# The end of a top-k spread over all 128 partitions, and its mask moved by four transfers

## The chip, the cores and the metric

The kernel runs on one core of a Trainium2 chip. The metric is the device time of one execution in microseconds (us); the median over runs is compared.

## The reference

One step of a decoder layer for 512 prompt tokens and for 32 new tokens of 8 sequences (4 each, the "samples") that have 1024 cached keys. Two attention branches read the same normed input and are merged by gates; a feed-forward network follows. The change is in branch A, for the samples:

```
rel   = relu(einsum('bthe,bse->bths', q_i, k_i))
score = einsum('bth,bths->bts', w_i, rel) * IDX_DIM**-0.5
score = where(causal, score, -inf)
_, idx = top_k(score, 256)        # at ties the lower index wins
s = einsum('btcgd,btncd->btcgn', qg, kv_a[idx][..., 0]) * HEAD_DIM**-0.5
p = softmax(where(valid, s, -inf));  o = einsum('btcgn,btncd->btcgd', p, kv_a[idx][..., 1])
```

The kernel gathers nothing: it makes a mask over all 1056 keys of a row (1024 cached and 32 new ones), 0 for a chosen key and -1e30 for any other, adds it to the logits and takes the softmax over all.

## The kernel before, in words

The program is written as streams of small pieces, and a scheduler with a timeline of its own sets the order of the instructions on each engine from them. That order is fixed in the program: each engine takes its instructions in turn, and one that waits holds all behind it. In the stretch that matters (160 to 585 us of the span) three streams run side by side:

- **heads**: branch B and then branch A for the prompt, in units of one head and 128 query rows with 128, 256, 384 or 512 keys (a unit is named by its keys below). A unit of branch B is a product on PE into the PSUM bank `z` (L902), two sigmoids on ACT (`g` and `b`, L906, L907), a running product on DVE along `g` (L909), a product on POOL (L910), transposes on PE into `tp` (L825), copies on ACT and DVE (L828, L829) and the value product on PE (L838).
- **samples**: branch B for the samples in two groups of four sequences, then branch A. A group of branch B turns and splits keys (L992, L997, L998), makes logits on PE (L1021) and sums their parts into `zr` (`half` on ACT, L969; sum on DVE, L971). When the logits of the last keys are there, `weights` adds a mask to `zr` (L1045, DVE), takes sigmoids (L1047, L1048, ACT), a running product over 1056 keys (L1050, DVE) and a product (L1051, POOL); PE turns `zr` (L1058), ACT and DVE split it (L1065, L1066), and the value products follow (L1089), whose pages are split by ACT (L1082) and by DVE or POOL (L1083). Branch A for the samples comes last (`dsa_sample`): in `products` the mask is added to the logits by a matmul with the selector `rowsel` (L1149).
- **dense**: projections with weights in two parts, three matmuls to a product (L464), into the PSUM bank `mm`, emptied by ACT (`rowy`, L500). The weights are split by ACT (L116) and POOL (L119).

The banks `z` and `mm` exist once each: whoever wants one waits until the reader of the last value is done. SP issues the page loads (`kb`, `vb`, L375), the weight loads (L106) and the loads of the heads, in turn.

**The top-k.** The score `score_s` lies on 32 partitions, one row of 1056 keys each. Four transfers lay it out as `score4` on 128 partitions, 264 keys each (L591). Thirty-two rounds find the least chosen score bit by bit: a count per partition on DVE (L596), a matmul with `group` into `z` that adds the four counts of a row (L598), and two small operations on DVE (L600, L605 or L607). The streams interleave with these rounds. The end (L610 to L620) goes back to `score_s` on 32 partitions: which keys equal the least score (L612), which are greater and how many (L613), how many places are left (L614), a running count of the equal ones (L615), those of them that fit (L616), the sum (L617), and the mask in two pieces (L618 and L620). The mask is written with the cached keys in another order, so that `products` reads 256 neighbouring elements.

## Time and profile before

| what | value |
|---|---|
| median of 3 runs | 1070.34 us (1068.96 to 1074.01) |
| the profiled execution, its own time | 1067.42 us |
| its span, first to last instruction | 1065.6 us |
| busy: PE, DVE, ACT, POOL | 92%, 70%, 50%, 44% of the span |
| PE busy from 160 to 585 us | 386.31 of 425 us |

All times of instructions are from the profiled execution, in us from the start of its span. A row of a timeline has the start, the duration, the engine, the line, the operation, what it writes and reads, and in brackets the idle time of its engine before it and what ended that. PE is TensorE's matmuls, PEld its weight loads, DVE VectorE, ACT ScalarE, POOL GpSimd, SP the engine that issues most transfers. Matmuls overlap: what a matmul costs PE is the distance between starts. The granted clock of TensorE is given as a share of full speed.

### The profile page before, as it was taken

What the parts mean: (1) busy time and instruction counts of PE and PEld (TensorE: products, weight loads), DVE (VectorE), ACT (ScalarE), POOL (GpSimd) and SP (SyncE); (2) the same over time, 40 slices, a digit from 0 to 9 for tenths busy, and PEclk for the clock granted to TensorE, in tenths of its full rate; (3) what the DMA queues carried; (4) which work ended last, traced back from release to release, by engine and by line L of the source; (5) the groups of instructions that cost most, each with busy time, mean ns of one, the idle gap of its engine ahead of it and who ended that gap; (6) DMA issues with size and microseconds to landing.
All of it is one profiled execution on the core that took longest, in us unless ns stands there. A gap on an engine that the chain in (4) does not pass through costs nothing.

```text
span 1065.6 us, 20642 instructions
## 1 busy us (share of the span) xinstructions
PE 984.7 (92%) x7446; PEld 931.0 (87%) x7446; DVE 740.7 (70%) x1441; ACT 531.2 (50%) x1020; POOL 469.9 (44%) x413
## 2 busy tenths in 40 slices
PE   6899998787989996999999799979999999999995
PEld 5899998776669996888888799979999999999995
DVE  4468995798997786578784976787787876513233
ACT  6234535574556564677785544534444444423223
POOL 4555545226763236652635834411323232545441
PEclk9999999998999998999998999989999999999998
DMA  9775547886767765864525663223432341223222
GB/s 269 181 205 169 152 121 228 250 253 174 228 209 242 223 188 165 256 218 144 193 72 181 201 179 90 71 71 89 119 100 83 97 119 43 75 88 90 83 82 85
DMA packets 184704, 162.15 MB, mean 152 GB/s; under 512 B 13338, under 2 KB 148058, under 8 KB 183578
## 3 DMA queue, kind: packets, MB, share of 16 engines
q1 hardware_dynamic: 176410, 140.00, 45.5%
q0 software_dynamic: 1872, 10.75, 2.9%
q10 hardware_dynamic: 6320, 10.08, 2.9%
q8 instruction: 59, 0.97, 0.4%
q14 instruction: 43, 0.35, 0.1%
HBM read 133.37 MB, written 22.01 MB: 146 GB/s over the span
## 4 chain that ended last, share of the span: by engine, by line
PE 52%; DVE 11%; issue 7%; POOL 5%; DMA 4%; ACT 2%; SPq 1%; ACTq 0%; DVEq 0%; POOLq 0%
PE mm L464 8%; PE ffB L1553 8%; PE acc L1607 6%; PE ffC L1553 5%; PE ffA L1553 5%; POOL wl L119 4%; PE z L1607 3%; PE mm L1607 3%; PE acc L1021 2%; PE ts L992 2%; PE acc L1089 2%; DVE g L909 1%; DMA vb<-in_cache_kv_b 1%; PE tp L825 1%; PE tp L838 1%
## 5 line engine op out<-in xcount | busy, mean ns | idle before, releaser
L119 POOL TENSOR_TENSOR wl<-wst,wh 128x512 fp32r<-128x512 f32 (+2 forms) x198 | 228.8, 1177 | 193.8 <-ACT wh L116 193.8
L464 PE MATMUL mm<-xh,wh 128*128 128x256 f32 (+2 forms) x484 | 145.7, 301 | 9.3 <-ACT rowy L500 5.5
L464 PE MATMUL mm<-xh,wl 128*128 128x256 f32 (+2 forms) x484 | 141.6, 293 | 2.4 <-POOL wl L119 2.4
L464 PE MATMUL mm<-xl,wh 128*128 128x256 f32 (+2 forms) x484 | 142.5, 294 | 0.0
L116 ACT ACTIVATE wh<-wst 128x1024 fp32r<-128x1024 f32 (+3 forms) x99 | 88.6, 895 | 103.0 <-PE z L1607 42.1
L227 POOL TENSOR_TENSOR wl<-wst,wh 128x512 fp32r<-128x512 f32 x40 | 59.9, 1519 | 164.4 <-ACT wh L224 164.4
L464 PEld LDWEIGHTS mm<-xh,wh 128*128 128x128 f32 (+1 forms) x484 | 93.1, 192 | 21.0 <-issue 7.3
L464 PEld LDWEIGHTS mm<-xh,wl 128*128 128x128 f32 (+1 forms) x484 | 93.1, 192 | 3.4 <-POOL wl L119 2.6
L464 PEld LDWEIGHTS mm<-xl,wh 128*128 128x128 f32 (+1 forms) x484 | 93.0, 192 | 0.5
L224 ACT ACTIVATE wh<-ws 128x1024 fp32r<-128x1024 f32 x40 | 42.4, 1061 | 68.5 <-PE ffC L1553 36.1
L1607 PE MATMUL acc<-actp,wh 128*128 128x256 f32 (+1 forms) x352 | 68.1, 289 | 0.0
L910 POOL TENSOR_TENSOR b<-b,g 128x127 f32<-128x127 f32 (+3 forms) x32 | 28.4, 887 | 82.8 <-DVE g L909 43.0
L229 DVE TENSOR_TENSOR wl<-ws,wh 128x1024 fp32r<-128x1024 f32 x40 | 52.1, 1301 | 6.0 <-ACT wh L224 6.0
L1607 PEld LDWEIGHTS acc<-actp,wh 128*128 128x128 f32 x352 | 55.4, 188 | 0.1
L998 DVE TENSOR_TENSOR kl<-ts,kh 128x512 fp32r<-128x512 f32 x64 | 43.4, 686 | 16.2 <-ACT kh L997 15.5
L464 PE MATMUL acc<-xh,wh 128*128 128x256 f32 (+1 forms) x176 | 51.3, 293 | 3.1 <-DVE gt L1407 2.7
L464 PE MATMUL acc<-xh,wl 128*128 128x288 f32 (+1 forms) x176 | 51.4, 293 | 0.0
L464 PE MATMUL acc<-xl,wh 128*128 128x288 f32 (+1 forms) x176 | 51.0, 291 | 0.0
L1607 PE MATMUL acc<-actp,wl 128*128 128x256 f32 (+1 forms) x176 | 49.9, 288 | 1.2 <-POOL wl L119 1.2
L997 ACT ACTIVATE kh<-ts 128x512 fp32r<-128x512 f32 x64 | 38.0, 602 | 23.9 <-PE ts L992 20.1
L1083 POOL TENSOR_TENSOR vl<-vb,vh 128x512 fp32r<-128x512 f32 x24 | 36.6, 1529 | 28.0 <-ACT vh L1082 24.9
L1082 ACT ACTIVATE vh<-vb 128x512 fp32r<-128x512 f32 x64 | 38.4, 626 | 20.6 <-DMA vb<-in_cache_kv_b 13.0
(438 smaller groups left out, 3433.7 us busy)
## 6 DMA issues: line engine op xcount, KB each, us to landing
wst<-in_w_in SPq DMA_DIRECT2D x38, 512.0 KB, 4.3
kb<-in_cache_kv_b SPq DMA_DIRECT2D x64, 256.0 KB, 4.6
vb<-in_cache_kv_b SPq DMA_DIRECT2D x64, 256.0 KB, 4.0
wst<-in_w_ffn_gate SPq DMA_DIRECT2D x40, 256.0 KB, 3.0
wst<-in_w_ffn_up SPq DMA_DIRECT2D x40, 256.0 KB, 3.4
wst<-in_w_ffn_down SPq DMA_DIRECT2D x16, 384.0 KB, 3.6
wst<-in_w_ffn_down SPq DMA_DIRECT2D x16, 320.0 KB, 3.2
gate_d<-rowy ACTq DMA_DIRECT2D x16, 272.0 KB, 4.2
```

The costliest lines, as they stand in the source:

```text
L116: self.nc.scalar.activation(h, st, AF.Copy)
L119: self.nc.gpsimd.tensor_sub(l[:, k], st[:, k], h[:, k].bitcast(F32))
L224: self.nc.scalar.activation(h, src, AF.Copy)
L227: self.nc.gpsimd.tensor_sub(l[:, g], src[:, g], h[:, g].bitcast(F32))
L229: self.nc.vector.tensor_sub(l, src, h.bitcast(F32))
L464: nc.tensor.matmul(ps, ww[:, k, :m], aa[:, k, hs], start=(k == 0 and p == 0), stop=(k == nk - 1 and p == 2))
L997: nc.scalar.activation(kh[:, :, :2 * P], tpv, AF.Copy)
L998: nc.vector.tensor_sub(kl[:, :, :2 * P], tpv, S(kh[:, :, :2 * P]))
L1082: nc.scalar.activation(vh, raw, AF.Copy)
L1083: (nc.vector if pg % 3 else nc.gpsimd).tensor_sub(vl, raw, S(vh))
L1553: nc.tensor.matmul(ps[:, g], ww[:, g, k, :], aa[:, k, :], start=(first and k == 0 and p == 0), stop=(k == 3 and p == 2), skip_group_check= ...
L1607: nc.tensor.matmul(ps, ww[:, k - ks[0], :], aa[:, hs], start=(k in (DOWN[0][0][0], DOWN[1][0][0]) and p == 0), stop=(k + 1 in (DOWN[0][1][ ...
```

## The change

The end of the top-k stays on `score4`: greater and equal keys are counted on 128 partitions of 264 keys each, two matmuls into `z` add the greater ones of all four parts of a row (`group`) and the equal ones of the parts before one's own (`before`, a new constant), and the number of places left (`room`) is read from `z`. The running count, the choice, the sum and the mask follow on 264 keys, and four transfers on SP's queue put the mask back on 32 partitions in `mask_s`, with the keys in the score's order. So `products` now reads the cached keys' mask with a step of 8 elements, after the four other matmuls instead of before them, and the new keys' mask by a matmul of its own. The constants' load is 128 columns wider.

```diff
+    before = group * (ii[:, None] // NS < ii[None, :] // NS)
...
-    c = np.concatenate([causal, causal_pos, newm, sbnew.reshape(P, -1), (ii % 16)[:, None], pages, strict, rowsel.reshape(P, -1), group], axis=1)
+    c = np.concatenate([causal, causal_pos, newm, sbnew.reshape(P, -1), (ii % 16)[:, None], pages, strict, rowsel.reshape(P, -1), group, before], axis=1)
...
-    cmb = xp.tile([P, 6 * P], F32, name="cmb")
+    cmb = xp.tile([P, 7 * P], F32, name="cmb")
...
-    group = cpool.tile([P, P], F16, name="group")
-    nc.gpsimd.tensor_copy(group, cmb[:, 5 * P:])
+    counts = cpool.tile([P, 2, P], F16, name="counts")
+    nc.gpsimd.tensor_copy(counts.rearrange("p a b -> p (a b)"), cmb[:, 5 * P:])
+    group, before = counts[:, 0, :], counts[:, 1, :]
...
-    tied_s = wk.tile([NS, NKEY], U8, name="tied_s")
+    tied4 = wk.tile([P, part], U8, name="tied4")
+    mask4 = wk.tile([P, part], BF16, name="mask4")
...
-        least, rank_s = cand[:NS].bitcast(F32), mask_s.bitcast(F16)
-        more = cpool.tile([NS, 2], F32, name="more")
-        nc.vector.tensor_scalar(tied_s, score_s, least, None, op0=OP.is_equal)
-        nc.vector.tensor_scalar(score_s, score_s, least, None, op0=OP.is_gt, op1=OP.add, accum_out=more[:, 0:1])
-        nc.vector.tensor_scalar(more[:, 1:2], more[:, 0:1], -1.0, float(NSEL), op0=OP.mult, op1=OP.add)
-        nc.vector.tensor_tensor_scan(rank_s, tied_s, tied_s, 0.0, OP.add, OP.bypass)
-        nc.vector.scalar_tensor_tensor(tied_s, rank_s, more[:, 1:2], tied_s, op0=OP.is_le, op1=OP.mult)
-        nc.vector.tensor_add(score_s, score_s, tied_s)
-        nc.vector.tensor_scalar(mask_s[:, :PAST].rearrange("q (j k) -> q k j", j=8),
-                                score_s[:, :PAST].rearrange("q (k j) -> q k j", j=8), -NEG, NEG, op0=OP.mult, op1=OP.add)
-        nc.vector.tensor_scalar(mask_s[:, PAST:], score_s[:, PAST:], -NEG, NEG, op0=OP.mult, op1=OP.add)
+        least, more4, rank4 = cand.bitcast(F32), ge4, mask4.bitcast(F16)
+        cnt = [cpool.tile([P, 1], F16, tag="cnt", name="cnt", bufs=2) for _ in range(2)]
+        nc.vector.tensor_scalar(more4, score4, least, None, op0=OP.is_gt, op1=OP.add, accum_out=cnt[0])
+        nc.vector.tensor_scalar(tied4, score4, least, None, op0=OP.is_equal, op1=OP.add, accum_out=cnt[1])
+        ps = zb()[:, :1]
+        nc.tensor.matmul(ps, group, cnt[0], start=True, stop=False)
+        nc.tensor.matmul(ps, before, cnt[1], start=False, stop=True)
+        room = cpool.tile([P, 1], F32, name="room")
+        nc.vector.tensor_scalar(room, ps, -1.0, float(NSEL), op0=OP.mult, op1=OP.add)
+        nc.vector.tensor_tensor_scan(rank4, tied4, tied4, 0.0, OP.add, OP.bypass)
+        nc.vector.scalar_tensor_tensor(tied4, rank4, room, tied4, op0=OP.is_le, op1=OP.mult)
+        nc.vector.tensor_add(more4, more4, tied4)
+        nc.vector.tensor_scalar(mask4, more4, -NEG, NEG, op0=OP.mult, op1=OP.add)
+        for g in range(4):
+            nc.sync.dma_start(mask_s[:, g * part:(g + 1) * part], mask4[g * NS:(g + 1) * NS, :])
...
-            nc.tensor.matmul(z[:, :w], rowsel[:NS, p, :], mask_s[:, c * 2 * P:c * 2 * P + w], start=True, stop=False)
             for b in range(2):
                 for v, t in enumerate((kh, kl)):
-                    nc.tensor.matmul(z[:, :w], stat[p % 2][:, b, :], t[:, b, :w], start=False, stop=(b + v == 2))
+                    nc.tensor.matmul(z[:, :w], stat[p % 2][:, b, :], t[:, b, :w], start=(b + v == 0), stop=(b + v == 2))
+            nc.tensor.matmul(z[:, :2 * P], rowsel[:NS, p, :],
+                             mask_s[:, :PAST].rearrange("q (k j) -> q j k", j=8)[:, 2 * c:2 * c + 2, :], start=False,
+                             stop=True, skip_group_check=True)
+            if c == 3:
+                nc.tensor.matmul(z[:, 2 * P:w], rowsel[:NS, p, :], mask_s[:, PAST:], start=False, stop=True,
+                                 skip_group_check=True)
```

The scheduler lays the streams out anew from the costs that it assumes, so the order changes between about 100 and 600 us on all engines. DVE in the program before, from the running product of the unit with 384 keys to the mask (line numbers of before; `tied_s`, `score_s` and `mask_s` belong to the top-k, `zr` and `sbg` to the samples' weights of the second group, `g` to the heads):

```order
L909 SCALAR_TENSOR_TENSOR g<-g 128x384
L614 TENSOR_SCALAR more<-more 32x1
L971 TENSOR_TENSOR zr<-acc,half 64x288
L616 SCALAR_TENSOR_TENSOR tied_s<-mask_s,more,tied_s 32x1056
L1045 TENSOR_TENSOR zr<-zr,masks 128x32
L909 SCALAR_TENSOR_TENSOR g<-g 128x512
L617 TENSOR_TENSOR score_s<-score_s,tied_s 32x1056
L1050 SCALAR_TENSOR_TENSOR sbg<-sbg 128x1056
L618 TENSOR_SCALAR mask_s<-score_s 32x128x8
L620 TENSOR_SCALAR mask_s<-score_s 32x32
L829 TENSOR_TENSOR pt<-tp,pt 128x3x128
```

The same place on DVE in the changed program. Its lines are numbered higher there: L978 is L971 of before, L1052 is L1045, L1057 is L1050, L916 is L909, L836 is L829; L615 to L625 are the new end of the top-k, with `ge_266` the greater keys, `tied_267` the equal ones and `mask_268` the running count and then the mask:

```order
L615 TENSOR_SCALAR ge_266,cnt<-score_265,cand 128x264
L616 TENSOR_SCALAR tied_267,cnt<-score_265,cand 128x264
L978 TENSOR_TENSOR zr<-acc,half 64x288
L622 SCALAR_TENSOR_TENSOR mask_268<-tied_267 128x264
L1052 TENSOR_TENSOR zr<-zr,masks 128x32
L1057 SCALAR_TENSOR_TENSOR sbg<-sbg 128x1056
L916 SCALAR_TENSOR_TENSOR g<-g 128x384
L621 TENSOR_SCALAR room<-z 128x1
L623 SCALAR_TENSOR_TENSOR tied_267<-mask_268,room,tied_267 128x264
L836 TENSOR_TENSOR pt<-tp,pt 128x2x128
L624 TENSOR_TENSOR ge_266<-ge_266,tied_267 128x264
L625 TENSOR_SCALAR mask_268<-ge_266 128x264
```

The heads' units 384 and 512 have moved behind the samples' weights, and `room`, which reads the bank `z`, stands behind the running products of the samples and of unit 384. PE in the changed program, at the two counting matmuls (L618, L619; L832 is L825 of before, L909 and L910 are L902 and L903, L466 is L464):

```order
L832 MATMUL tp<-ident,b 128x128 x2
L466 MATMUL mm<-xl,wh 128x288
L618 LDWEIGHTS counts
L618 MATMUL z<-cnt,counts 128x1
L619 LDWEIGHTS counts
L619 MATMUL z<-cnt,counts 128x1
L909 MATMUL z<-kk,qq 128x512 x2
L910 LDWEIGHTS identb
L910 MATMUL z<-mb,identb 128x128
L466 MATMUL mm<-xh,wh 128x256
```

Behind the last row 23 more dense matmuls stand, and then the transposes of `zr`. The product of unit 512 is the next to use `z` after the counts, so on PE it, and all behind it, waits for `room` on DVE. Before, that product stood ahead of everything shown of DVE, and 72 dense matmuls and the transposes of units 384 and 512 lay between it and the transposes of `zr`.

## The prediction

> **What bounds the kernel now.** I read the page first, then the busy times by stage, then who waited for whom on PE, and then the timelines of the stretch where PE stood.
>
> ```profile
> PE 984.7 (92%) x7446; PEld 931.0 (87%) x7446; DVE 740.7 (70%) x1441; ACT 531.2 (50%) x1020; POOL 469.9 (44%) x413
> ```
>
> PE is busy 92% of the span, so time is gained only where PE stands, or where it is given less to do. The busy times by stage (columns: stage in us, its length, busy time of PE, weight loads, DVE, ACT and POOL, granted clock, DMA share, GB/s) show where it stands: the stage with the end of the top-k, the like stage of the samples' first group, where no top-k ends, and all that follows until the streams are done.
>
> ```profile
> 388.00:420.00 32.00, 22.39 (x166) 21.43 (x165) 26.79 (x30) 14.50 (x27) 21.25 (x11) 0.89 0.50 155
> 238.00:262.00 24.00, 16.65 (x122) 16.03 (x122) 20.60 (x36) 11.81 (x26) 15.18 (x13) 0.86 0.62 173
> 426.00:585.00 159.00, 154.39 (x1085) 134.60 (x1084) 111.59 (x325) 115.09 (x271) 80.81 (x79) 0.97 0.57 176
> ```
>
> PE lacks 9.6 us in the first, and only 4.6 us in the 159 us behind it: what is gained in the first is handed on nearly whole. The waits of PE from 385 to 440 us, and the rows around the longest:
>
> ```profile
> PE tp L825 <- DVE pt L829: 6.3, 1, 6.3
> PE mm L464 <- ACT rowy L500: 3.6, 3, 2.6
> ```
> ```profile
> 412.41 1.09 PE L825 MATMUL tp<-ident,b 128*128 128x128 f32 x4 [6.34 <-DVE pt L829]
> ...
> 413.51 0.41 PE L464 MATMUL mm<-xh,wl 128*128 128x256 f32 x1
> 413.72 0.41 PE L464 MATMUL mm<-xl,wh 128*128 128x256 f32 x1
> ...
> 415.43 0.28 PE L464 MATMUL mm<-xh,wl 128*128 128x256 f32 x1
> 415.55 0.28 PE L464 MATMUL mm<-xl,wh 128*128 128x256 f32 x1
> ```
>
> After the wait the matmuls start 0.21 us apart instead of 0.12 until 415.43: nine starts, 9 x 0.09 = 0.8 us lost to the clock. What PE waited for stands in DVE's timeline:
>
> ```profile
> 389.63 0.76 DVE L612 TENSOR_SCALAR tied_s<-score_s,cand 32x1056 uint8<-32x1056 f32 x1
> ...
> 391.25 1.29 DVE L613 TENSOR_SCALAR_CACHE_REDUCE score_s<-score_s,cand 32x1056 f32<-32x1056 f32 x1
> ...
> 392.48 2.34 DVE L615 TENSOR_TENSOR_SCAN mask_s<-tied_s 32x1056 f16<-32x1056 uint8 x1
> ...
> 398.05 0.45 DVE L971 TENSOR_TENSOR zr<-acc,half 64x288 f32<-64x288 f32 x1
> 398.53 1.49 DVE L616 SCALAR_TENSOR_TENSOR tied_s<-mask_s,more,tied_s 32x1056 uint8<-32x1056 f16 x1
> ...
> 401.12 1.21 DVE L909 TENSOR_TENSOR_SCAN g<-g 128x512 f32<-128x512 f32 x1
> 402.25 2.26 DVE L617 TENSOR_TENSOR score_s<-score_s,tied_s 32x1056 f32<-32x1056 f32 x1
> 404.44 2.34 DVE L1050 TENSOR_TENSOR_SCAN sbg<-sbg 128x1056 f32<-128x1056 f32 x1
> 406.71 3.25 DVE L618 TENSOR_SCALAR mask_s<-score_s 32x1024 bf16<-32x1024 f32 x1
> 409.58 2.22 DVE L620 TENSOR_SCALAR mask_s<-score_s 32x32 bf16<-32x32 f32 x1
> 411.72 0.54 DVE L829 TENSOR_TENSOR pt<-tp,pt 128x384 fp32r<-128x384 f32 x1
> ```
>
> The seven large operations of the top-k's end take 13.6 us, and L829, for which PE stood, is queued right behind the last of them. L620 takes 2.22 us for 32 elements, and ends with POOL's product:
>
> ```profile
> 403.36 4.30 POOL L910 TENSOR_TENSOR b<-b,g 128x511 f32<-128x511 f32 x1
> 407.63 4.14 POOL L1051 TENSOR_TENSOR zr<-zr,sbg 128x1055 f32<-128x1055 f32 x1
> ```
>
> It starts at 409.58, POOL's L1051 ends at 411.77 and L620 at 411.80: DVE was held by POOL here. So the price of this place is 3.6 + 6.3 us of waits and 0.8 of clock: **10.7 us**.
>
> **Part 1, the end on 128 partitions.** The rows for its prices, and for those of the way to `room` (the last two list every run of a line: shortest, median and longest):
>
> ```profile
> L596 DVE TENSOR_SCALAR_CACHE_REDUCE ge<-score,cand 128x264 uint8<-128x264 f32 x32 | 15.5, 485 | 0.8
> ```
> ```profile
> 394.64 0.63 ACT L1082 ACTIVATE vh<-vb 128x512 fp32r<-128x512 f32 x1 [1.79 <-PE acc L1021]
> 395.30 0.41 ACT L969 ACTIVATE half<-acc 64x288 f32<-64x288 f32 x1
> ...
> 401.22 1.08 ACT L1047 ACTIVATE sbg<-zr 128x1056 f32<-128x1056 f32 x1 [3.16 <-DVE zr L1045]
> ```
> ```profile
> 395.93 2.03 DVE L909 TENSOR_TENSOR_SCAN g<-g 128x384 f32<-128x384 f32 x1
> ```
> ```profile
> L1045 DVE TENSOR_TENSOR zr<-zr,masks x2: 169/706/1242, 244.2 to 399.9; 128x32 f32<-128x32 f32 x2
> ```
> ```profile
> L909 DVE TENSOR_TENSOR_SCAN g<-g x32: 413/953/4840, 177.4 to 401.1; 128x128 f32<-128x128 f32 x8, 128x256 f32<-128x256 f32 x8, 128x384 f32<-128x384 f32 x8, 128x512 f32<-128x512 f32 x8
> ```
>
> The two counts cost 2 x 0.49 (L596 has their shape), the running count, the choice and the sum a quarter of 2.34, 1.49 and 2.26 (together 1.5), the mask about 0.3: 2.8 us on DVE instead of 13.6. But **the waits are not removed, they are replaced**. The counts are added in the bank `z`, and `room`, which frees it, is queued on DVE behind the sum into `zr`, L1045, the running product over 1056 keys and that of unit 384. Unit 512's product, next on PE and in `z`, cannot start before, nor the dense matmuls behind it. From the last logits of the samples the way to `room` is: a split that waits for the same logits 0.63, `half` 0.41, sum 0.45, running count 0.6, L1045 0.2 (its short run), L1047 1.08, L1050 2.34, unit 384's running product 1.2 (at most unit 512's time, undisturbed), `room` 0.15 (my estimate for one element). That is 7.1 us, and 7.5 with nine steps that each start some 0.05 after their releaser. Meanwhile PE has 24 dense matmuls at 0.12 (2.9), unit 384's product and two transposes (about 0.6): 3.5. So it stands 7.5 - 3.5 = 4.0 us. With L1045 at 1.24 and unit 384 at 2.03 it is 5.9; were a running product held as long as the 4.84 in the last row, 4.84 - 1.2 + 1.0 more, 8.6. Without the split and with half the steps' delays it is 3.2. I take 4.5 and 0.6 of clock (0.8 x 4.5/6.3): **5.1 us**, where 10.7 stood. What else hung on the place goes along: the product L1051 needs the same L1050, takes 4.14 at most as above and falls beside `room` and the 2.9 us of dense matmuls, so the transposes of `zr` wait little.
>
> **Part 2, the four transfers.** They stand on SP after the 42nd of the 64 value pages, wait for the mask, and behind them are a weight load, a head's output and the later pages. Four issues and a landing are bounded by those of the layout:
>
> ```profile
> L591 SPq DMA_DIRECT2D score<-score_s x4: 507/518/592, 176.5 to 183.3; - x4
> ...
> DMA to landing us min/median/max: 3.7/3.7/3.7
> ```
> ```profile
> L1149 PE MATMUL acc<-mask_s,mb x16: 277/278/292, 464.2 to 550.0; 32*128 32x256 bf16 x12, 32*128 32x288 bf16 x4
> ```
>
> 4 x 0.52 + 3.7 = 5.8 us after the mask, which I expect near 405 us, so 411; the mask is first read at 464. That distance, some 50 us, hides them; without it they would cost the 5.8. The pages behind them wait for buffers that are freed only after the transposes of `zr`, so 0 for these, and at most 2.1 us of issues. I take 0.
>
> **Part 3, the mask read with a step of 8.** Sixteen matmuls read 256 columns with the step, four more read 32 columns. No row shows such a read on PE. From below it is the row above: 0.28 us long like a dense one of that width, so 0.12 from start to start and nothing added. From above it is DVE's L618, which reads with the same step in f32: 3.25 us for 1024, so 0.81 for 256 and 0.69 more, 16 x 0.69 = 11 us. A gain has no reason. L618 is another engine's and was held by POOL in part, so I stay near the lower row and take half the pace, 0.1 more each: **+1.6 us**, on the path, since PE is full there (154.39 of 159 us). The Trainium skill, "SBUF — State Buffer", section "SBUF: two separate sides", speaks against this edit: accesses should hit a 16-byte line at least twice, and each that goes to a new line pays a penalty; eight bf16 elements are just one line. It gives no price; no run here shows it yet. The four small matmuls cost between 0.12 and 0.28 each in place of 32 columns of a wide one: **+0.5**. Moving the mask's matmul to the end of its group costs nothing by itself: PE does the same before ACT may read.
>
> **Part 4, the wider constants.** A quarter of 256 KB, 64 KB, at the 269 GB/s of the first slice is **+0.2 us** if the weight load behind it on SP is late by as much, 0 if not; the wider cast on POOL lies beside PE's work there.
>
> ```profile
> GB/s 269 181 205 169 152 121 228 250 253 174 228 209 242 223 188 165 256 218 144 193 72 181 201 179 90 71 71 89 119 100 83 97 119 43 75 88 90 83 82 85
> ```
>
> **Part 5, the order elsewhere.** Nearly all rows between 100 and 600 us are shuffled, with the same work. The largest wait that can come or go with that is the one of the first group's stage:
>
> ```profile
> PE z L598 <- DVE ge L596: 5.6, 1, 5.6
> ```
>
> The count L596 is queued there behind the running product that took 4.84 where the shortest took 0.41. The same streams meet there in the new order too, so I take 0, with 4.4 us to either side.
>
> **The sum.** -10.7 + 5.1 + 1.6 + 0.5 + 0.2 = -3.3 us. Against the profiled execution's own 1067.42 that is 1064.1; the median of the runs shown, 1070.34, is 2.9 above that execution, so the median forecast is **1067.0 us**. A measurement of this kernel can tell about 0.5%, 5.4 us, from no change, so this counts as within 0.5%.
>
> **The rivals.**
>
> *The whole wait goes (0.30).* PE finds unit 512's operands and `room` early, as the sum into `zr` is no longer held up by the top-k. For it: most of the 9.9 us of waits came through DVE's queue, which gets 10.8 us lighter. Against: the row order above. With a step that costs nothing it gives -10.7 + 0.5 + 0.2 = -10.0, so 1060.3.
>
> *The new wait is as long as the old (0.15).* A running product ahead of `room` is held by POOL. For it: 4.84 us in the first group, L620 here. It gives 8.6 us of wait and 0.9 of clock instead of 5.1, so 1071.4, no change. The Trainium skill, "SBUF — State Buffer", section "Who interferes with whom", has the rule: a DVE instruction with two SBUF inputs and a POOL instruction that reads SBUF exclude each other, and the loser waits for the whole instruction. L620's end with L1051 agrees.
>
> *The mask's reads are slow (0.13), the slower side.* PE reads a step of 8 as DVE did in L618, 0.81 us for 256 columns, in a stage in which PE has no slack. For it: L618 is the only row with that step. Against: POOL held part of it. The price is 11 instead of 1.6 us: -3.3 + 9.4 = +6.1, so 1076.4. It decides from (5.4 + 3.3 + 1.6)/16 = 0.64 us more for each matmul on.
>
> **How the numbers follow.** The forecast has 0.42. Its own range is 1061 to 1074: the wait from 3.2 to 8.6, the step, and the other stages to either side. Faster by over 0.5% is the first rival and a 0.02 of the forecast, 0.32; slower is the last and 0.01, 0.14; the rest, 0.54, is within. The range that holds 8 in 10 reaches from the first rival's 1060 to 1075, and leaves out the last rival and the tails.
>
> **What would show it.** Right: the seven rows become about 2.8 us of DVE; PE's longest wait near 400 us is that of a `z` product for `room`, 4 to 6 us; PE is full behind it; the mask's matmuls lie about 0.1 us further from the next start. Wrong: no wait for `room`, or one over 8 us; reads of the mask 0.5 us apart or more; or another wait of 4 us or more between 160 and 585 that takes the gain back.

## The result and the profile after

| what | before | after |
|---|---|---|
| median | 1069.65 us (1066.3 to 1074.01) | 1085.58 us (1080.58 to 1086.31) |
| ratio of after to before, 95% interval | | 1.0141 (1.0121 to 1.016) |
| profiled execution, own time and span | 1067.42 and 1065.6 us | 1080.77 and 1079.0 us |

The changed kernel is **slower by 1.4%**, 15 us; forecast was 1067.0, with a range that ended at 1075. In the profiled executions the spans differ by 13.4 us. Each ratio, here and in the experiments, compares fast runs of a kernel with fast runs of before from the same session, so it need not be the quotient of two medians of a table, and one execution of e18, of 3278.74 us, is left out of its ratio. Times of the changed kernel are in its own line numbers: 1 higher than in before up to about L360, 2 higher up to about L555, 3 up to the top-k's end, 7 above it and 12 behind `products` (L909 is L902 of before, L945 is L938, L1065 is L1058, L1159 is L1149).

The busy times of the engines on the page of after, to be held against the same line of before:

```profile
PE 991.7 (92%) x7452; PEld 933.5 (87%) x7452; DVE 735.6 (68%) x1441; ACT 530.8 (49%) x1020; POOL 464.0 (43%) x413
```

PE has 7 us more of busy time, half of the loss; the other half is time in which it stands. The busy times by stage (columns as before) of after: the stage of the top-k's end, the one behind it, and the long stage of the streams.

```profile
388.00:420.00 32.00, 27.41 (x191) 25.34 (x189) 24.12 (x40) 17.81 (x36) 14.35 (x11) 0.89 0.42 125
440.00:460.00 20.00, 10.62 (x62) 9.71 (x61) 4.68 (x13) 7.36 (x16) 5.46 (x6) 0.74 0.86 220
426.00:585.00 159.00, 147.12 (x1011) 124.54 (x1010) 103.83 (x309) 105.56 (x251) 73.34 (x71) 0.96 0.56 166
```

In before the second of these was full:

```profile
440.00:460.00 20.00, 20.00 (x132) 16.40 (x130) 16.14 (x39) 15.23 (x36) 10.42 (x9) 1.00 0.83 264
```

So the stage that the forecast was about did gain: PE is busy 27.41 us there instead of 22.39. Then 9.4 us are missing between 440 and 460, at a clock of 0.74. Four rows of waits of PE in after say which waits these are: two from 385 to 440 us, one from 440 to 480, and one from the first 120 us that before does not have.

```profile
PE z L618 <- ACT b L914: 2.3, 1, 2.3
PE z L909 <- DVE room L621: 2.2, 1, 2.2
...
PE z L945 <- DMA qqa<-qa_d: 8.9, 1, 8.9
...
PE tp L822 <- DMA khh<-rowh: 3.0, 1, 3.0
```

The first two are the bank `z` at the top-k's end, the third is branch A's first product, which stands for its own operands. SP's queue shows why these are late. After:

```profile
418.77 10.03 SPq L377 DMA_DIRECT2D vb<-in_cache_kv_b  x8
...
429.67 0.93 SPq L377 DMA_DIRECT2D vb<-in_cache_kv_b  x2
430.65 1.33 SPq L878 DMA_DIRECT2D kaa<-ka_d  x2
432.03 0.60 SPq L1349 DMA_DIRECT2D vv<-va_d  x1
432.67 4.72 SPq L883 DMA_DIRECT2D qqa<-qa_d  x4
```

Before:

```profile
420.67 1.32 SPq L871 DMA_DIRECT2D kaa<-ka_d  x2
422.04 0.82 SPq L1337 DMA_DIRECT2D vv<-va_d  x1
422.90 1.72 SPq L876 DMA_DIRECT2D qqa<-qa_d  x2
424.88 6.74 SPq L375 DMA_DIRECT2D vb<-in_cache_kv_b  x5
```

The order laid out anew has put the loads `kaa` and `qqa` behind 52 of the 64 value pages, where 42 stood ahead of them, so they are issued 10 us later, and `qqa` takes long to land beside the pages (the chain of work that ended last has this piece):

```profile
433.62 17.92 DMA qqa<-qa_d
```

Where the three streams then stand, by the first and last start of three lines on PE: the transposes of the samples' weights, branch A's first and last products, and the last transposes of the samples. Before:

```profile
L1058 PE MATMUL ts<-ident,zr x16: 270/272/297, 260.2 to 418.0; 128*128 128x128 f32 x16
...
L938 PE MATMUL z<-kaa,qqa x64: 221/336/501, 434.2 to 554.7; 128*128 128x128 f32 x16, 128*128 128x256 f32 x16, 128*128 128x384 f32 x16, 128*128 128x512 f32 x16
...
L1218 PE MATMUL ts<-stacked,oa x32: 272/273/293, 512.0 to 572.9; 64*128 64x32 f32 x32
```

After:

```profile
L1065 PE MATMUL ts<-ident,zr x16: 270/273/273, 259.4 to 413.0; 128*128 128x128 f32 x16
...
L945 PE MATMUL z<-kaa,qqa x64: 220/338/504, 451.6 to 571.8; 128*128 128x128 f32 x16, 128*128 128x256 f32 x16, 128*128 128x384 f32 x16, 128*128 128x512 f32 x16
...
L1230 PE MATMUL ts<-stacked,oa x32: 272/273/294, 519.9 to 586.0; 64*128 64x32 f32 x32
```

Behind the top-k's end the changed kernel is 5.0 us ahead (413.0 against 418.0). Branch A starts 17.4 us late, takes as long as before (120.2 against 120.5 us), and the streams end 13.1 us late. The rest of the program only hands that on.

The new end of the top-k on DVE (rows of other work left out), which forecast had at 2.8 us:

```profile
399.30 0.49 DVE L615 TENSOR_SCALAR_CACHE_REDUCE ge<-score,cand 128x264 uint8<-128x264 f32 x1
...
399.71 0.48 DVE L616 TENSOR_SCALAR_CACHE_REDUCE tied<-score,cand 128x264 uint8<-128x264 f32 x1
...
400.72 0.89 DVE L622 TENSOR_TENSOR_SCAN mask<-tied 128x264 f16<-128x264 uint8 x1
...
405.97 0.13 DVE L621 TENSOR_SCALAR room<-z 128x1 f32<-128x1 f32 x1
406.14 2.05 DVE L623 SCALAR_TENSOR_TENSOR tied<-mask,room,tied 128x264 uint8<-128x264 f16 x1
...
408.44 0.75 DVE L624 TENSOR_TENSOR ge<-ge,tied 128x264 uint8<-128x264 uint8 x1
409.23 1.25 DVE L625 TENSOR_SCALAR mask<-ge 128x264 bf16<-128x264 uint8 x1
```

They add up to 6.0 us. The four transfers and the mask's reads on PE follow:

```profile
L627 SPq DMA_DIRECT2D mask_s<-mask x4: 572/588/590, 410.5 to 412.4; - x4
...
DMA to landing us min/median/max: 1.8/1.8/1.8
```
```profile
L1159 PE MATMUL acc<-mask_s,mb x16: 603/606/609, 486.4 to 563.1; 32*128 32x256 bf16 x16
```

A read with the step takes 0.606 us where the neighbouring one took 0.278. From its start to the next one's PE loses 0.53 us instead of 0.21; first after, then before:

```profile
486.36 0.60 PE L1159 MATMUL acc<-mask_s,mb 32*128 32x256 bf16 x1
486.89 0.66 PE L1142 MATMUL ts<-ident,kav 128*128 128x128 f32 x4
```
```profile
484.80 0.28 PE L1149 MATMUL acc<-mask_s,mb 32*128 32x256 bf16 x1
485.01 0.39 PE L1152 MATMUL acc<-kah,qap 128*128 128x256 f32 x1
```

### The profile page after: what moved, and what is told of

Its sections match the earlier page's. It is cut to its first block, busy times and chain, and to the rows that moved or that the text cites. A ratio compares the mean times of both kernels' runs of the same rounds, so it can differ in the third digit from the quotient of the medians.

```text
span 1079.0 us, 20672 instructions
## 1 busy us (share of the span) xinstructions
PE 991.7 (92%) x7452; PEld 933.5 (87%) x7452; DVE 735.6 (68%) x1441; ACT 530.8 (49%) x1020; POOL 464.0 (43%) x413
## 4 chain that ended last, share of the span: by engine, by line
PE 61%; DVE 12%; DMA 8%; issue 7%; POOL 4%; SPq 3%; ACT 2%; ACTq 1%; DVEq 0%; POOLq 0%
PE mm L466 11%; PE ffB L1565 8%; PE acc L1619 6%; PE ffC L1565 5%; PE ffA L1565 5%; POOL wl L120 3%; PE acc L466 3%; PE z L1619 3%; PE mm L1619 3%; PE acc L1096 2%; PE acc L1028 2%; PE tp L845 2%; PE ts L999 2%; DMA qqa<-qa_d 2%; PE z L466 2%
## 5 line engine op out<-in xcount | busy, mean ns | idle before, releaser
L120 POOL TENSOR_TENSOR wl<-wst,wh 128x512 fp32r<-128x512 f32 (+2 forms) x198 | 224.4, 1155 | 199.4 <-ACT wh L117 190.8
L466 PE MATMUL mm<-xh,wh 128*128 128x256 f32 (+2 forms) x484 | 147.6, 305 | 4.7 <-DVE gt L1419 2.6
L466 PE MATMUL mm<-xh,wl 128*128 128x256 f32 (+2 forms) x484 | 143.8, 297 | 1.5 <-POOL wl L120 1.5
L466 PE MATMUL mm<-xl,wh 128*128 128x256 f32 (+2 forms) x484 | 143.5, 296 | 0.0
L466 PEld LDWEIGHTS mm<-xh,wh 128*128 128x128 f32 (+1 forms) x484 | 95.1, 196 | 10.0 <-DVE gt L1419 2.8
L466 PEld LDWEIGHTS mm<-xh,wl 128*128 128x128 f32 (+1 forms) x484 | 94.6, 196 | 3.7 <-POOL wl L120 1.7
L466 PEld LDWEIGHTS mm<-xl,wh 128*128 128x128 f32 (+1 forms) x484 | 94.3, 195 | 0.8
L466 PE MATMUL acc<-xh,wh 128*128 128x288 f32 (+1 forms) x176 | 51.2, 294 | 0.6 <-DVE gt L1419 0.6
L466 PE MATMUL acc<-xh,wl 128*128 128x288 f32 (+1 forms) x176 | 51.2, 293 | 0.0
L466 PE MATMUL acc<-xl,wh 128*128 128x288 f32 (+1 forms) x176 | 51.2, 292 | 0.0
L999 PE MATMUL ts<-ident,kb 128*128 128x128 f32 x256 | 41.2, 279 | 4.5 <-DVE kl L1005 2.4
```

The costliest lines, as they stand in the source:

```text
L120: self.nc.gpsimd.tensor_sub(l[:, k], st[:, k], h[:, k].bitcast(F32))
L466: nc.tensor.matmul(ps, ww[:, k, :m], aa[:, k, hs], start=(k == 0 and p == 0), stop=(k == nk - 1 and p == 2))
L999: nc.tensor.transpose(tp[:, (2 * j + pg) * P:(2 * j + pg + 1) * P], V["kp"][pg][:, (2 * jj + j) * P:(2 * jj + j + 1) * P], ident)
```

## The experiments

Two theories were put against each other. **Order**: the operations of the change are worth little either way, and the time is lost because the scheduler laid all streams out anew. **Operations**: the strided reads and the counts in `z` make the loss, whatever the order. In the table, "pages" is how many value pages stand ahead of `kaa` on SP, and "branch A" is the first and last start of its products on PE in the profiled execution. That execution is one run, and not always a typical one: in after it took 1080.77 us and in e18 1069.47, both 5 under the median, in e10 1081.41, 8 above it. In e4 ACT issues the loads, so no pages stand ahead of them in its queue.

| run | median us | ratio to before, 95% interval | pages | branch A |
|---|---|---|---|---|
| before | 1069.65 | | 42 | 434.2 to 554.7 |
| after | 1085.58 | 1.0141 (1.0121 to 1.016) | 52 | 451.6 to 571.8 |
| e1 before, wide constants | 1082.03 | 1.0128 (1.0099 to 1.0157) | 46 | 451.9 to 578.0 |
| e9 the same, load on ACT's queue | 1069.27 | 1.0021 (1.0002 to 1.004) | 42 | 435.0 to 555.3 |
| e2 before, strided reads | 1069.85 | 1.0013 (0.9993 to 1.0032) | 42 | 429.5 to 557.9 |
| e5 before, mask written by ACT | 1067.94 | 0.9998 (0.9978 to 1.0018) | 42 | 428.5 to 553.6 |
| e12 before, rounds later | 1081.33 | 1.0135 (1.0097 to 1.0173) | 50 | 447.6 to 569.4 |
| e18 before, dense work sooner | 1074.17 | 1.0041 (1.0015 to 1.0068) | 43 | 436.9 to 552.7 |
| e4 after, loads on ACT's queue | 1087.32 | 1.0181 (1.0152 to 1.0211) | | 451.5 to 582.7 |
| e8 after, rounds sooner | 1084.3 | 1.0148 (1.0112 to 1.0185) | 46 | 448.2 to 560.8 |
| e14 after, heads sooner | 1082.01 | 1.0106 (1.0085 to 1.0128) | 41 | 429.9 to 564.8 |
| e17 after, contiguous reads | 1077.69 | 1.0063 (1.0041 to 1.0085) | 52 | 454.5 to 570.1 |
| e3 after, constant apart | 1076.47 | 1.0089 (1.0056 to 1.0121) | 43 | 425.4 to 561.9 |
| e6 e3 and contiguous reads | 1075.49 | 1.0064 (1.004 to 1.0089) | 43 | 429.4 to 561.9 |
| e7 e6 and counts in `ts` | 1063.25 | 0.9937 (0.9918 to 0.9957) | 39 | 427.4 to 550.8 |
| e11 e7, rounds sooner | 1064.16 | 0.996 (0.9937 to 0.9983) | 39 | 419.9 to 549.3 |
| e15 e7, strided reads | 1065.53 | 0.9963 (0.9945 to 0.9981) | 39 | 427.2 to 552.6 |
| e10 after, counts in `ts` | 1073.64 | 1.0062 (1.004 to 1.0084) | 38 | 431.4 to 562.1 |
| e13 e10, load on ACT's queue | 1077.65 | 1.0073 (1.005 to 1.0096) | 39 | 430.4 to 559.0 |
| e16 e13, contiguous reads | 1072.48 | 1.0019 (1.0003 to 1.0035) | 39 | 430.6 to 553.7 |

### The wider constants alone (e1, e9)

e1 is before with the constants' load and cast 128 columns wider, and nothing that uses them; e9 moves that load to ACT's queue.

```diff
-    cmb = xp.tile([P, 6 * P], F32, name="cmb")
+    cmb = xp.tile([P, 7 * P], F32, name="cmb")
-    nc.sync.dma_start(cmb, c_masks[:, 3 * P + 3 * NS + 1:])
+    nc.scalar.dma_start(cmb, c_masks[:, 3 * P + 3 * NS + 1:])     # e9 only
```

> The kernel before, with the wider constants' load and cast alone (part 4 of the change); the top-k's end and the mask's reads are those of before. The scheduler lays the order out anew from this alone: SP's queue has a weight load ahead of the loads of khh again, and the loads of the heads' branch A stand behind 46 value pages (42 before, 52 in the changed kernel). Theory A (the loss is mostly the order that was laid out anew): 3 to 10 us slower than before, with PE's wait for khh of about 3 us near 70 us. Theory B (the loss is the new operations: strided reads and the counts in z): no change, within 2 us.

> The first experiment again (before with the wider constants and the wider cast, which took 1082.0 us), but the load is issued by ACT instead of SP. The width is the same; PE's order from about 60 us on is that of before, with khh ahead of the weight load and kaa behind 42 value pages. Theory of the order: the 12.5 us go, 1069 to 1071. If the wider load or cast itself cost the time: 1079 or more.

Measured: 1.28% slower, and 0.2%. The same bytes and the same cast cost some 12 us on one queue and about 2 on the other, so neither the bytes nor the cast cost them. On SP's queue the load moves the scheduler's timeline: a weight load goes ahead of `khh`, and from there on every stream is laid out otherwise, with branch A at 451.9 us; on ACT's queue PE's order from about 60 to 564 us is that of before. Theory A had expected 3 to 10 us.

### The place of the top-k's end and the reads, in the order of before (e2, e5)

e5 keeps before's order on PE; e2 keeps it up to the mask's matmuls, near 464 us, which stand elsewhere in their groups. e2 writes the mask in the score's order with one DVE operation and reads it with the step; e5 lets ACT write it in page order and reads neighbours.

```diff
-        nc.vector.tensor_scalar(mask_s[:, :PAST].rearrange("q (j k) -> q k j", j=8), ...)
-        nc.vector.tensor_scalar(mask_s[:, PAST:], score_s[:, PAST:], -NEG, NEG, op0=OP.mult, op1=OP.add)
+        nc.vector.tensor_scalar(mask_s, score_s, -NEG, NEG, op0=OP.mult, op1=OP.add)      # e2
+        nc.scalar.activation(mask_s[:, :PAST].rearrange("q (j k) -> q j k", j=8),         # e5
+                             score_s[:, :PAST].rearrange("q (k j) -> q j k", j=8), AF.Copy, bias=NEG, scale=-NEG)
+        nc.scalar.activation(mask_s[:, PAST:], score_s[:, PAST:], AF.Copy, bias=NEG, scale=-NEG)
```

> The kernel before, with the mask written in the score's order in one operation on 32 partitions, and read by the sixteen matmuls with a step of 8 elements at the end of their groups, and by four small ones. The rest of the order is that of before (42 value pages ahead of the loads of branch A, khh ahead of the weights). Theory A: each strided matmul costs 0.32 us more and each small one 0.13, 5 to 6 us in all on a full PE: 4 to 6 us slower. Theory B (the reads and new waits make up the loss alone): 9 us or more slower. A third reading (the streams have slack for it): no change.

> The kernel before, with one edit: the two DVE operations that write the mask (3.25 and 2.22 us in before) are two operations on ACT that write the same mask in page order; reads by TensorE stay contiguous, the order of PE's instructions is that of before. Both theories hold that the place of the top-k's end is worth about 5 us, as it was in the run with strided reads (PE stood 2.8 us instead of 6.3 there, the end of the zr transposes came 5 us earlier) and that the strided reads gave that back. So about 1064.5 us, ratio 0.993 to 0.997, with PE's wait for L829's copy 2 to 3 us. If instead the reads cost nothing and the 5 us at the place were lost later to something else, it stays at 1069 to 1070.

Measured: both the same as before. That misses both theories of e2 and hits its third reading, and e5 misses its 0.993 to 0.997. In e5 the place did become shorter, by 6.3 us at the last transposes of `zr` (418.0 in before):

```profile
L1058 PE MATMUL ts<-ident,zr x16: 270/272/296, 260.0 to 411.7; 128*128 128x128 f32 x16
```

Yet the streams' last transposes come only 0.8 us earlier (572.1 against 572.9). PE's waits in e5 from 405 to 480 us show where most of it went:

```profile
PE tp L825 <- DVE sm L945: 2.6, 1, 2.6
PE tp L825 <- DVE tmp L843: 1.7, 1, 1.7
PE z L938 <- DMA qqa<-qa_d: 0.4, 1, 0.4
```

Before had 0.3 us of the first of these there and none of the others. They are branch A's start: its first product comes 5.7 us earlier, then PE waits for the softmax on DVE, and the branch takes 125.1 us instead of 120.5. The difference between e2 and e5, 0.15% or 1.6 us, holds the step, the four small matmuls and the other way of writing the mask together; within the intervals it is nothing.

### The order of the kernel before, disturbed (e12, e18)

Nothing is computed otherwise; one number of the list that shares out the work is changed.

```diff
-TK_N = 80
+TK_N = 78          # e12
-D_COST = 174
+D_COST = 168       # e18
```

> The kernel before, every operation kept, with the top-k's rounds handed out 2.5% later (78 for 80): the order is laid out anew from about 160 us on, kaa stands behind 50 value pages instead of 42. Theory of the order: the late loads of branch A cost as in the changed kernel, a wait of several us of PE for qqa or kaa near 440 us, 1074 to 1082. If what is computed decides: 1069 to 1071.

> The kernel before, every operation kept, with the dense stream given 168 instead of 174 in the list that shares out the work: the order is laid out anew from about 160 us on, but branch A's loads stay where they are (behind 43 value pages instead of 42). If the place of branch A's loads is what decides between orders: 1066 to 1072. If any other order than that of before loses: 1075 or more.

Measured: 1.35% and 0.41% slower. e12, without one operation of the change, repeats its picture: `kaa` behind 50 pages, a transfer for which branch A's first product stands, and a late branch A.

```profile
PE z L938 <- DMA vb<-in_cache_kv_b: 6.1, 1, 6.1
```
```profile
L938 PE MATMUL z<-kaa,qqa x64: 218/338/794, 447.6 to 569.4; 128*128 128x128 f32 x16, 128*128 128x256 f32 x16, 128*128 128x384 f32 x16, 128*128 128x512 f32 x16
```

An order can thus cost as much as the whole change did. e18 keeps the loads early and loses 0.41%, 4 us, all the same, which is neither of the outcomes expected of it.

### The changed kernel's order, disturbed (e4, e8, e14)

```diff
-        twice(S(kaa)..., ka_d...)
+        twice(S(kaa)..., ka_d..., nc.scalar)                       # e4, and qqa of the first unit
-TK_N = 80
+TK_N = 82                                                          # e8
-H_COST = 65
+H_COST = 73                                                        # e14
```

> The changed kernel, with the loads of kaa and of the first head's query for branch A issued by ACT in place of SP, so that they don't stand behind ten value pages in SP's queue. Theory A: PE's wait of 8.9 us for qqa near 443 us goes or falls under 3 us, and the kernel gains 6 to 10 us against the changed one, to about 1077. Theory B: no change, since the wait is made up elsewhere, 1083 to 1086. A third reading (the transfers share the same bandwidth whatever the queue): the wait stays over 6 us.

> The changed kernel with every operation kept; the top-k's rounds are handed out 2.5% sooner (82 instead of 80 to a share), which lays the order out anew from about 160 us on: branch A's loads stand behind 46 value pages instead of 52. Theory of the order: PE's wait of 8.9 us for qqa shrinks to 2 or 3 and the time falls to 1074 to 1082. Theory of the operations: 1085 to 1087, as the changed kernel.

> The changed kernel with every operation kept (counts in z, wide load on SP, strided reads); the heads' stream is given 73 instead of 65 in the list that shares out the work, so that branch A's loads stand behind 41 value pages instead of 52. If the late start of branch A is what cost the changed kernel its time: the first product of branch A comes before 440 us and the time falls by 8 or more, to 1070 to 1077. If the counts in z cost it whatever the order: 1083 to 1088.

Measured: 1087.3, 1084.3 and 1082.0, against 1085.6. The wait for `qqa` is gone in all three, and others stand in its place: in e8 one of 10.4 us for ACT's `rowy`, in e4 two of 4.1 and 3.6. None of the three came out in a range expected of it. e4 hardly made the loads earlier: ACT issued `kaa` at 428.28 instead of 430.65 and `qqa` at 431.98 instead of 432.67, and branch A starts at 451.5 as in after. So e4 is no test of early loads; e8 and e14 are. In e14 branch A starts at 429.9, earlier than in before, and takes 134.9 us instead of 120.2:

```profile
L945 PE MATMUL z<-kaa,qqa x64: 221/337/689, 429.9 to 564.8; 128*128 128x128 f32 x16, 128*128 128x256 f32 x16, 128*128 128x384 f32 x16, 128*128 128x512 f32 x16
```

So the late loads are what PE waits for in the changed kernel, but **not alone the cause**: issuing them earlier brought 1.3 us (e8) and 3.6 us (e14) in the medians, each in a new order, and my expectation of 8 or more fell.

### Constant apart, contiguous reads, another bank (e3, e6, e7, e11)

e3 loads the new constant by itself much later; e6 also turns the mask on the 128 partitions, so that PE reads neighbours; e7 also counts in a bank of `ts`, of which there are two; e11 is e7 with the rounds sooner.

```diff
+    bef = hp.tile([P, P], F32, name="bef")                                           # e3, later in the program
+    nc.sync.dma_start(bef, c_masks[:, 9 * P + 3 * NS + 1:])
+    nc.gpsimd.tensor_copy(before, bef)
+        turned4 = mask4[:, :part].rearrange("p (j k) -> p j k", j=8)                 # e6
+        nc.vector.tensor_scalar(turned4, more4.rearrange("p (k j) -> p j k", j=8), -NEG, NEG, op0=OP.mult, op1=OP.add)
+        nc.vector.tensor_scalar(mask4[3 * NS:, part:], more4[3 * NS:, part - NS:], -NEG, NEG, op0=OP.mult, op1=OP.add)
-        ps = zb()[:, :1]
+        ps = lts()[:, :1]                                                            # e7
```

> The changed kernel, with the matrix before loaded and cast apart, late and off the early queue, so that the wide load is undone. All of the new end, its four transfers and the strided reads stay. The order laid out for it is like that of before: khh ahead of the weights, 43 value pages ahead of the loads of branch A. Theory A: the loss of 14 to 15 us shrinks to 0 to 4 (new end -4, strided reads +5.7). Theory B: nothing that it names is removed, so 1083 to 1086 again.

> The changed kernel with the new constant loaded apart (1076.5 us) and the mask turned into page order on the 128 partitions before the transfers, so TensorE's mask reads are contiguous and the four small matmuls are gone; one small DVE operation and one transfer more. Both theories price the strided reads at 16 x 0.32 + 0.5 = 5.6 us, so 1071. If it is over 1075, the strided reads were hidden and the order lost the time; if it is under 1069, the new operations were the whole loss.

> As the run before (contiguous reads, constant apart), and the two counting matmuls write a bank of ts instead of z, so unit 512's product does not wait for room. Theory of the operations (their waits and reads are the loss, the order is neutral): 4.5 us less than the run before, about 1066.5. Theory of the order (what is laid out anew decides): the wait for room in z goes, but the order changes again between 160 and 585 us (kaa behind 39 value pages instead of 43), so anything from 1062 to 1076, and the difference to the run before does not equal the wait removed.

> The run of 1063.25 us (constants apart, contiguous reads, counts in ts) with the top-k's rounds handed out 2.5% sooner (82 for 80), which lays PE's order out anew from about 160 us on; kaa stays behind 39 value pages. If that run was fast by luck of its order: 1066 to 1075. If its bank was the reason: 1061 to 1066.

Measured: 1076.5, 1075.5, 1063.25 and 1064.2. e3 fell between its two theories. e6 was expected at 1071 and gained 1.0 us in the medians where 5.6 were priced, so the strided reads' price did not come through there; its order on PE differs from e3's. e7 is **the fastest kernel here, 0.6% under before**, and e11, in another order, stays close to it.

The change from e6 to e7 brought 12 us where the wait for `room` was priced at 4.5. But e6 has no wait for `room` to remove. These are all the waits of PE that the profile lists in e6 from 385 to 440 us:

```profile
PE tp L837 <- POOL b L922: 2.5, 2, 1.5
PE z L950 <- DVE mx L953: 2.5, 1, 2.5
PE tp L837 <- DVE sm L957: 2.3, 1, 2.3
PE ts L1070 <- POOL zr L1063: 1.4, 1, 1.4
PE z L950 <- DMA qqa<-qa_d: 1.0, 1, 1.0
PE mm L466 <- ACT rowy L502: 0.9, 2, 0.5
```

In e6 `room` is read at 394.4 us and the next product into `z` starts only at 396.19; e3, too, has no such wait. What differs is branch A: it takes 132.5 us in e6, with 6.8 us of waits for `mx` on DVE and a granted clock of 0.92 from 426 to 585 us, and 123.4 us in e7, with 1.9 and 0.98. So the 12 us are not a wait in `z`; they came with the order that the scheduler laid out for the other bank.

### The bank and the reads in the changed kernel (e10, e13, e15, e16, e17)

e10 is after with the counts in `ts`; e13 also loads the constants on ACT's queue. e15 gives e7's reads the step, e16 takes it from e13's, e17 from the changed kernel's. In these three the order of every engine stays word for word, so each prices the step alone; these kernels read other keys' mask and leave out the right choice of keys.

```diff
-            nc.tensor.matmul(..., mask_s[:, :PAST].rearrange("q (k j) -> q j k", j=8)[:, 2 * c:2 * c + 2, :], ...)
+            nc.tensor.matmul(..., mask_s[:, c * 2 * P:(c + 1) * 2 * P].rearrange("q (j k) -> q j k", j=2), ...)   # e16, e17
```

> The changed kernel with one edit: the two counting matmuls write a bank of ts instead of z. Wide load on SP's queue, strided reads and four small matmuls as in the changed kernel; kaa then stands behind 38 value pages instead of 52, the weight load still ahead of khh. Theory that counts in z (the wait for room, and the scheduler's answer to it, which moves unit 512 and the branch A loads back) carry most of the loss: 12 us less than the changed kernel, as e7 was 12 less than e6: 1071 to 1076. Theory that the wider load carries it: 1080 to 1084.

> The changed kernel with two edits: the counts in a bank of ts, and the constants' load issued by ACT, so that the weight load no longer stands ahead of khh. Reads with the step of 8 and the four small matmuls are kept; kaa stands behind 39 value pages, as in the run of 1063.25 us, which differs from it only in the reads (and in which queue loads the constant). If the strided reads are hidden in part, as between the two kernels with the order of before (1069.85 against 1067.94): 1064 to 1066. If each start to start difference of 0.32 us comes through whole: 1068 to 1070. If the run with counts in ts and the load on SP (1073.6) was slow for another reason than its early order: 1072 or more.

> The run of 1063.25 us (constants apart, contiguous reads, counts in ts) with only the address pattern of 12 of the 16 mask reads changed to a step of 8 (so they read other keys' mask than they should; the four wider ones stay contiguous). The order of every engine is the same, word for word. If the reads cost what they cost between the two kernels with the order of before (1.9 us for 16): 1064 to 1066. If 12 x 0.32 comes through whole: 1067. If they are what made the run of 1077.65 slow: 1072 or more.

> The run of 1077.65 us (changed kernel, counts in ts, constants loaded by ACT) with only the pattern of the sixteen mask reads changed to neighbouring elements (so they read other keys' mask than they should); the four small matmuls and the order of every engine stay, word for word. If the order is what made that run slow: 1074 to 1077. If the strided reads did: 1063 to 1067.

> The changed kernel with only the pattern of the sixteen mask reads changed to neighbouring elements (so they read other keys' mask than they should); its order stays word for word. It gives the price of the step in the changed kernel itself. Theory of the order: 1080 to 1084, 2 to 5 us less than the changed kernel. Theory that the reads carry the loss: 1072 or less.

Measured for the bank: after to e10, 1.0141 to 1.0062, about 0.8%, as expected of the bank, and again in a new order: the 4.5 us of waits in `z` are gone, and `kaa` stands behind 38 pages instead of 52. e13, with the load off SP, has no early wait for `khh` and is no faster than e10, so that wait is not what held e10 at 1073.6. Measured for the step, as differences of the ratios times 1070 us: 2.8 us in e7's order (12 reads), 5.8 in e13's and **8.3 in the changed kernel's**, each uncertain by some 3 us by the intervals. e15 came out at 1065.5, in the first of its ranges; e16 and e17 fell between their theories. The row of the reads in e17, which has the same order as after:

```profile
L1159 PE MATMUL acc<-mask_s,mb x16: 277/278/278, 488.9 to 561.8; 32*128 32x256 bf16 x16
```

Sixteen times 0.32 us is 5.1, and twelve times 3.8; all three differences agree with that within their intervals. That the step counts for more in one order than in another is therefore not shown. Between e7 and e16 no read has the step and all counts are in `ts`; the 9 us that remain there are the four small matmuls (0.12 us each in the changed kernel), the turning of the mask on DVE and its one more transfer, the way in which the constants are loaded, and differences of order.

## Why the prediction was wrong

**What bounds the kernel.** That a gain at the top-k's end "is handed on nearly whole" failed. e5 has 6.3 us less there with the same order on PE, and the run is the same as before: branch A's start took it back. A PE that is busy 154.39 of 159 us was still not the bound there: as PE came earlier, waits for the softmax and `tmp` on DVE appeared that before did not have.

**Part 1, the end on 128 partitions.** The place went in the main as described. The waits in `z` are 2.3 + 2.2 = 4.5 us, as forecast, but that is in part luck: the forecast had all of it at unit 512's product, for `room`, and half stands at the counts, which wait for the bank's last reader on ACT. PE was 5.0 us ahead behind it, of a forecast 5.6; that is not shown to be the new end's work alone, since e12, with the old end in another order, has the same transposes done by 405.7. DVE's 2.8 us became 6.0, for the most part since L623 and L625 ran beside POOL's products, which cost PE no wait.

**Part 2, the four transfers.** Right: issued from 410.5, landed 1.8 us after the last was issued, some 72 us ahead of the first read at 486.4.

**Part 3, the reads with a step.** The mechanism was right, the size was not: +0.1 us each was +0.32 (1.6 us became 5.1 of PE's time), and the changed kernel without the step is 8.3 us faster, give or take 3. The rival of slow reads asked for 0.64 each; the sign of being wrong that the text gave, reads 0.5 us apart, did come, with 0.53. The four small matmuls cost 0.12 us each, so their +0.5 holds. The Trainium skill, "SBUF — State Buffer", section "SBUF: two separate sides", whose rule of two hits to a 16-byte line speaks against such a read, agrees in its sign; the price is the 0.606 us above, and no run here shows that the line is the reason.

**Part 4, the wider constants, +0.2 us.** As bytes that is not contradicted: e9 lies 0.2% above before, with an interval from 0.2 to 4 us. As a cause it failed: on SP's queue the load changed the order, and that alone was 1.28% in e1.

**Part 5, the order elsewhere, 0 ± 4.4 us.** This step of the sum failed worst. I took the largest single wait of the old order as the bound for a new one. What came was a new wait of 8.9 us for `qqa`, the text's own sign of being wrong, in an order that starts branch A 17.4 us late. The same operations in other orders measured 0.4% and 1.35% above before (e18, e12). The rows that I needed were in the order of SP: `kaa` behind 52 pages instead of 42 could be read there, and I weighed only the transfers that the change adds.

How the miss divides can be said only in part. Without the step (e17) the changed kernel is still 0.63%, 6.7 us, above before, with a wait of 7.6 us for `qqa`; the sum without Part 3 has it 4.9 us below. By e5 up to 5.6 of these 11.6 us can be Part 1's gain that was not handed on. The rest, some 6 us or more, is left to the order; that it is the order is argued from e1, e12 and e18, since no run has the changed kernel's operations in the order of before.

**The rivals.** The whole wait did not go, the new wait was not as long as the old, and the reads were slower than forecast but did not reach their rival's price. What the rival of a long wait said of L620 needs a correction: L620 reads one tensor, so its row says nothing of an operation with two inputs; the row of L623 at the end of this document does. What happened, a new order with waits of its own, was the tail of Part 5, to which the text gave 0.01. Settled: with before's own operations an order alone can cost 1.35%, some 14 us (e12), and the step costs PE 0.32 us a read, 8.3 us with an uncertainty of 3 in the changed kernel. Not settled: what the bank `ts` is worth by itself, since the two kernels that took it first (e7 and e10, 1.3% and 0.8% faster) got a new order with it and the first had no wait in `z` to lose; and which feature of an order makes it fast. Every kernel with `kaa` behind 46 pages or more took over 1077 us, but early loads alone did not bring the time down (e14, e13).

## What to carry to other kernels

Where a scheduler lays out the order from its own costs, an edit far from the hot place (here the width of one load, on one queue) can move more time than the edit one is pricing: compare the new order queue by queue, see what the first operands of the next stage now stand behind, and give the order a range taken from a few re-laid copies of the kernel before, not from its longest wait. A short step that borrows a bank which the next stage needs can hold that stage (4.5 us here, and nothing in another order): look in the new order for who is next to use it. A step in a read that PE makes is paid on every read (0.32 us here), so price it from a row, or write the data in the reader's order. A gain at one place is worth what the next chain lets through: look at what PE would wait for if it came six microseconds sooner.

## What the runs showed of the hardware

- A moving read of 256 bf16 columns with a step of 8 elements takes PE 0.606 us, against 0.278 for neighbours (start to next start 0.53 against 0.21).
- The same 128x264 DVE operations took 0.51 and 0.30 us in e14, and 2.05 and 1.25 in the changed kernel (L623 and L625). In e14:

```profile
409.21 0.51 DVE L623 SCALAR_TENSOR_TENSOR tied<-mask,room,tied 128x264 uint8<-128x264 f16 x1
...
410.22 0.30 DVE L625 TENSOR_SCALAR mask<-ge 128x264 bf16<-128x264 uint8 x1
```

  In the changed kernel POOL's product lay across the first of them (405.35 + 2.55 = 407.90, the held operation ends at 408.19), and POOL's weight split across the second (the first of its two ends near 410.3, L625 at 410.48):

```profile
405.35 2.55 POOL L1058 TENSOR_TENSOR zr<-zr,sbg 128x1055 f32<-128x1055 f32 x1 [4.30 <-ACT rowy L502]
...
408.87 2.75 POOL L120 TENSOR_TENSOR wl<-wst,wh 128x512 fp32r<-128x512 f32 x2
```

  The Trainium skill, "SBUF — State Buffer", section "SBUF: two separate sides", calls the pair of ports that DVE and POOL share an exclusive lock for a whole instruction; the rows of L623 and L1058 agree, the held operation ending just behind POOL's.
- `qqa` (four small loads) took 17.92 us until it had landed behind ten value pages issued from 418.77 on, at a DMA share of 0.86 from 440 us on.
